# Start addresses of the matrix operands in a two-block transformer kernel: weight tiles at 0 instead of 160, activations of 256 columns at 192 instead of 96 bytes modulo 256

## Chip, cores and metric

The kernel runs on one core of one Trainium2 chip. The metric is the device time of one execution in microseconds (us). Before the change the median of three runs is 2402.97 us (2402.97 to 2404.96).

## What is computed

The reference takes 256 tokens of width 1024 in float32 through two models, one after the other. The first has two layers, each with a feed-forward part, a mixer of three kinds of attention, and a second feed-forward part. The second model has two layers as well, with feed-forward parts, a neighbourhood attention with pooling, and a short convolution; its scale and shift vectors come from a conditioning vector. Cut to what matters here:

```python
D_MODEL, SEQ, D_FF = 1024, 256, 2816

def swiglu(h, w_gu, w_down):
    g, u = jnp.split(h @ w_gu, 2, axis=-1)
    return (jax.nn.silu(g) * u) @ w_down

for l in range(DEPTH):                                  # first model
    x = x + 0.5 * swiglu(rmsnorm(x, g_ffn1[l]), w_ffn1_gu[l], w_ffn1_down[l])
    x = x + hybrid_mixer(rmsnorm(x, g_mix[l]), w_in[l], ...)
    x = x + 0.5 * swiglu(rmsnorm(x, g_ffn2[l]), w_ffn2_gu[l], w_ffn2_down[l])

def ffn_sublayer(h, m, g, w13, w2, base):               # second model
    hn = modulate(rms_norm(h, g), m[:, :, base], m[:, :, base + 1])
    return h + 0.5 * m[:, :, base + 2] * swiglu_2(hn, w13, w2)
```

Eight feed-forward passes make up most of the time: four of the first model, four of the second. One of the second model's handles the 256 tokens and 256 context tokens together.

## The kernel before

**Layout.** Activations stand transposed: the feature lies on the 128 partitions, the 256 tokens (T) in the columns. Each weight block of 128x128 is the stationary operand, and the activations stream past it as the moving operand.

**Three products for one.** Weights and activations are split into a high part of type float32r and the remainder (whi and wlo, h.hi and h.lo). `mm3` (L309 to L313) issues three matmuls per block: high by high (L311), high by low (L312), low by high (L313). With eight blocks of 128 features, one pass over the input takes 24 matmuls. The hidden activations of the feed-forward part are kept in the same way in a tile named A, and those of the mixer in tiles named yy.

**Weights.** They stream from HBM in one order, 1 MB at a time, into three tiles named raw (`load`, L266). ScalarE rounds 1024 columns to whi (L288), VectorE subtracts to give wlo (L291), into four tiles of each. SyncE issues the transfers.

**Stages.** In `ffn`, the gate and up products are written to PSUM tiles named gu, and the down product, with A as the moving operand, to tiles named dn. In the mixers, `tblock` writes tiles named ps. The first model's input has 256 columns. The second model carries the shift vector as two additional columns (TX = 258), so its gu matmuls and part of its ps matmuls stream 258 columns. The joint pass of tokens and context streams 512 columns in dn. VectorE and ScalarE evacuate, and between them VectorE works on a list of dot products for the conditioning (tile mjunk, L553).

**Addresses.** `rows` (L378) makes the tile for an activation: it starts at a multiple of 256 bytes, and its first `at` floats stay unused. With `at` = 24 the data starts at 96 modulo 256. Inside the tile the high and low rows of each block follow each other. A row of 256 columns is 1024 bytes long, so every row starts at 96 modulo 256. A row of 258 columns is 1032 bytes long, so the high row of block k starts at 96 + 16k and the low row at 104 + 16k (k from 0 to 7): the high rows run through 96, 112, 128, 144, 160, 176, 192 and 208. The pool `strm` holds a small tile named one (L1070, L1075, L1076: set to ones and squared once at the start) ahead of raw, whi and wlo. It is 8 floats, 32 bytes, and leaves the tiles behind it at 160 modulo 256. A weight block is 512 bytes, so every block starts at 160 modulo 256 too.

The order of the instructions on each engine is set by a scheduler, from priorities that the code gives; addresses play no part in it.

Of the kernel before, what the change touches and what calls it, by code (L numbers as in the profile page):

```python
# [8 lines left out]
F32 = mybir.dt.float32  # L9
# [7 lines left out]
P = 128  # L17
T = 256
D = 1024
KB = 8  # L20
# [230 lines left out]
class Kern:  # L251
# [123 lines left out]
        nc.vector.tensor_tensor(t, t, v, op=OP.mult)  # L375
        nc.vector.scalar_tensor_tensor(y, t, 1.5, y, op0=OP.add, op1=OP.mult)

    def rows(self, pool, tag, k, n, at=24, **kw):  # L378

        m = 2 * k * n  # L380
        t = pool.tile([P, m + at], F32R, tag=tag, name=tag, align_bytes=256, **kw)
        return t[:, at:].rearrange("p (k s t) -> p k s t", k=k, s=2)

    def newh(self, n=T):
        return self.act(self.rows(self.hpool, "h", KB, n), n)

    def act(self, t, n=T):
        return Act(t[:, :, 0], t[:, :, 1], n, t)
# [662 lines left out]
    def run(self):  # L1051
# [9 lines left out]
        pool = lambda n, b, **k: tc.tile_pool(name=n, bufs=b, **k)  # L1061
        with pool("strm", self.SB) as self.strm, pool("const", 1) as cp, pool("h", 2) as self.hpool, \
# [4 lines left out]
            sc = None  # L1067
            sx.X = cp.tile([P, KB, T], F32, name="X")

            one = self.strm.tile([P, 8], F32, name="one", bufs=1)  # L1070
            self.colt = cp.tile([P, COLSW], F32, name="colt")
            nc.sync.dma_start(self.colt, self.a["cols"])
            self.norm_begin(sx, col("g_ffn1", 0, 8))
# [63 lines left out]
            for l in range(2):  # L1137
                for part in range(2):
# [22 lines left out]
                    n = f"{l}{part}"  # L1161
# [100 lines left out]
```

## Time and profile before

| what | value |
|---|---|
| median of three runs | 2402.97 us |
| the profiled execution's own time | 2412.81 us |
| its span, first to last instruction | 2411.0 us |
| TensorE busy with matmuls | 2375.8 us (99%), 18996 matmuls |
| VectorE busy | 1895.8 us (79%) |
| ScalarE busy | 1183.1 us (49%) |
| GpSimd busy | 185.8 us (8%) |
| weight transfers (queue 1) | 54.6% of 16 engines' span |
| mean granted TensorE clock | 0.996 of full speed |

The profiled execution is 9.8 us (0.4%) above the median of the runs. Matmuls overlap in the profile: one that lasts 282 ns is followed by the next after some 118 ns. So the busy share of TensorE says nothing of its rate. The rate is read from counts: a window of the trace counts every matmul that overlaps it, so the mean interval between two starts is the window plus one duration, divided by the count.

### The profile page before, as it was taken

Reading aid. Unit: us, or ns where it says so; the run is one execution under the profiler, and the core shown is the slowest. Engines: PE = TensorE matmul, PEld = TensorE weight load, DVE = VectorE, ACT = ScalarE, POOL = GpSimd, SP = SyncE. Lnnn points to the kernel's source line nnn. Section 1 sums busy time; section 2 is a strip of 40 time slices with the busy share of each in tenths; the row PEclk is TensorE's granted clock in tenths of the full one; section 3 lists DMA queues with packets and bytes.
Section 4 is the critical chain, followed back from the end, with each engine's and each line's share of the span. In section 5 each row is a group of like instructions: output and inputs, shape, how many; then the busy total and the mean of one; then the engine's idle time right before and its main releaser. Section 6 shows DMA issues by size and latency. Waiting matters only on the chain.

```text
span 2411.0 us, 46263 instructions
## 1 busy us (share of the span) xinstructions
PE 2375.8 (99%) x18996; PEld 2307.1 (96%) x18996; DVE 1895.8 (79%) x3244; ACT 1183.1 (49%) x1803; POOL 185.8 (8%) x283
## 2 busy tenths in 40 slices
PE   8999999999999999999999999999999999999998
PEld 8999899999999989899999899988899999999998
DVE  8876887997897678699787657685799799788773
ACT  5444455544544445465544323435655455545553
POOL 0001103000000110220110000030100000001000
PEclk9999999999999999999999999999999999999999
DMA  7655344675666534466545445353378778655553
GB/s 278 217 200 191 118 158 140 236 234 197 234 227 203 207 119 143 147 237 246 210 171 196 150 156 186 130 173 105 117 280 290 251 259 294 233 187 182 191 178 112
DMA packets 79012, 469.01 MB, mean 195 GB/s; under 512 B 8772, under 2 KB 11120, under 8 KB 33488
## 3 DMA queue, kind: packets, MB, share of 16 engines
q1 hardware_dynamic: 77344, 459.67, 54.6%
q0 software_dynamic: 1168, 5.86, 0.7%
q8 instruction: 149, 2.44, 0.4%
q14 instruction: 63, 0.52, 0.1%
q10 hardware_dynamic: 288, 0.52, 0.1%
HBM read 464.96 MB, written 1.06 MB: 193 GB/s over the span
## 4 chain that ended last, share of the span: by engine, by line
PE 94%; DVE 3%; ACT 2%; issue 1%; POOL 0%; DMA 0%; DVEq 0%; SPq 0%; ACTq 0%; POOLq 0%
PE gu L312 16%; PE gu L313 15%; PE gu L311 15%; PE dn L311 8%; PE dn L312 8%; PE dn L313 8%; PE ps L312 6%; PE ps L311 6%; PE ps L313 6%; PE y L316 2%; PE tok L316 1%; DVE wlo L291 1%; PE sc L316 1%; ACT whi L288 0%; PE zc L316 0%
## 5 line engine op out<-in xcount | busy, mean ns | idle before, releaser
L288 ACT ACTIVATE whi<-raw 128x1024 fp32r<-128x1024 f32 (+2 forms) x717 | 752.4, 1051 | 774.6 <-PE gu L312 271.3
L291 DVE TENSOR_TENSOR wlo<-raw,whi 128x1024 fp32r<-128x1024 f32 (+2 forms) x717 | 873.6, 1220 | 257.2 <-ACT whi L288 254.1
L311 PE MATMUL gu<-h,whi 128*128 128x258 f32 (+1 forms) x3168 | 893.3, 282 | 7.3 <-ACT whi L288 7.3
L312 PE MATMUL gu<-h,whi 128*128 128x258 f32 (+1 forms) x3168 | 896.9, 283 | 0.0
L313 PE MATMUL gu<-h,wlo 128*128 128x258 f32 (+1 forms) x3168 | 893.1, 282 | 0.9 <-DVE wlo L291 0.9
L311 PEld LDWEIGHTS gu<-h,whi 128*128 128x128 f32 x3168 | 598.0, 189 | 7.5 <-ACT whi L288 7.3
L313 PEld LDWEIGHTS gu<-h,wlo 128*128 128x128 f32 x3168 | 602.8, 190 | 1.3 <-DVE wlo L291 1.1
L312 PEld LDWEIGHTS gu<-h,whi 128*128 128x128 f32 x3168 | 600.8, 190 | 0.2
L311 PE MATMUL dn<-A,whi 128*128 128x256 f32 (+1 forms) x1408 | 414.8, 295 | 0.0
L313 PE MATMUL dn<-A,wlo 128*128 128x256 f32 (+1 forms) x1408 | 414.7, 295 | 0.0
L312 PE MATMUL dn<-A,whi 128*128 128x256 f32 (+1 forms) x1408 | 414.3, 294 | 0.0
L311 PE MATMUL ps<-h,whi 128*128 128x256 f32 (+1 forms) x1296 | 371.5, 287 | 9.2 <-DVE ev L917 4.2
L312 PE MATMUL ps<-h,whi 128*128 128x256 f32 (+1 forms) x1296 | 371.8, 287 | 0.1
L313 PE MATMUL ps<-h,wlo 128*128 128x256 f32 (+1 forms) x1296 | 367.7, 284 | 0.0
L312 PEld LDWEIGHTS dn<-A,whi 128*128 128x128 f32 x1408 | 266.1, 189 | 7.8
L313 PEld LDWEIGHTS dn<-A,wlo 128*128 128x128 f32 x1408 | 265.6, 189 | 7.9
L311 PEld LDWEIGHTS dn<-A,whi 128*128 128x128 f32 x1408 | 265.3, 188 | 7.8
L311 PEld LDWEIGHTS ps<-h,whi 128*128 128x128 f32 x1296 | 247.1, 191 | 13.3 <-issue 4.4
L312 PEld LDWEIGHTS ps<-h,whi 128*128 128x128 f32 x1296 | 247.8, 191 | 3.0 <-issue 1.7
L313 PEld LDWEIGHTS ps<-h,wlo 128*128 128x128 f32 x1296 | 248.1, 192 | 0.9 <-issue 0.4
L553 DVE SCALAR_TENSOR_TENSOR mjunk<-mraw,sc 128x1024 bf16<-128x1024 f32 x184 | 225.3, 1224 | 16.6 <-DMA mraw<-modw 16.4
L464 ACT ACTIVATE A<-av 128x256 fp32r<-128x256 f32 x198 | 80.9, 412 | 117.0 <-DVE av L521 58.4
(301 smaller groups left out, 2123.1 us busy)
## 6 DMA issues: line engine op xcount, KB each, us to landing
raw<-wst SPq DMA_DIRECT2D x344, 1024.0 KB, 4.9
mraw<-modw SPq DMA_DIRECT2D x144, 512.0 KB, 4.5
sc<-cc SPq DMA_DIRECT2D x7, 1024.0 KB, 6.8
raw<-wst SPq DMA_DIRECT2D x6, 714.0 KB, 4.1
raw<-wst SPq DMA_DIRECT2D x7, 512.0 KB, 4.4
raw<-wst SPq DMA_DIRECT2D x4, 869.0 KB, 4.5
k<-c POOLq DMA_DIRECT2D x2, 1026.0 KB, 7.5
bt<-rpb SPq DMA_DIRECT2D x8, 256.0 KB, 2.8
```

The lines of the kernel that those rows point to most:

```text
L288: i = nc.scalar.activation(hi[:, :w], raw, AF.Copy)
L291: i = nc.vector.tensor_tensor(lo[:, :w], raw, hi.bitcast(F32)[:, :w], op=OP.subtract)
L311: mm(ps, w[0], x[0], start=start, stop=False)
L312: mm(ps, w[0], x[1], start=False, stop=False)
L313: mm(ps, w[1], x[0], start=False, stop=stop)
L316: self.nc.tensor.matmul(ps, w, x, start=start, stop=stop)
L464: self.nc.scalar.activation(hi, src, AF.Copy)
L553: self.pin(nc.vector.scalar_tensor_tensor(junk, raw, 0.5, self.sc[:, c], op0=OP.mult, op1=OP.mult, accum_out=m[:, idx:idx + 1]))
```

## The change

Three constants change. `rows` leaves 48 floats unused instead of 24, so activations of 256 columns, A and yy start at 192 instead of 96 modulo 256. `newh` leaves 16 for inputs of 258 columns: their high rows start at 64 + 16k instead of 96 + 16k (64 to 176 instead of 96 to 208), their low rows at 72 + 16k instead of 104 + 16k. The tile one grows from 32 to 128 bytes, so all tiles behind it move by 96 bytes, and the weight tiles start at 0 instead of 160 modulo 256. Tiles of other kinds move by 96 bytes as well, except those that are aligned to 256 bytes.

The order of the instructions on every engine stays as it is. Two instructions at the start get larger: the memset and the activation on the tile one work on 32 columns instead of 8.

```diff
-    def rows(self, pool, tag, k, n, at=24, **kw):
+    def rows(self, pool, tag, k, n, at=48, **kw):
 
         m = 2 * k * n
         t = pool.tile([P, m + at], F32R, tag=tag, name=tag, align_bytes=256, **kw)
         return t[:, at:].rearrange("p (k s t) -> p k s t", k=k, s=2)
 
     def newh(self, n=T):
-        return self.act(self.rows(self.hpool, "h", KB, n), n)
+        return self.act(self.rows(self.hpool, "h", KB, n, 48 if n == T else 16), n)
...
-            one = self.strm.tile([P, 8], F32, name="one", bufs=1)
+            one = self.strm.tile([P, 32], F32, name="one", bufs=1)
```

## Rows read from the trace of the kernel before

**Rows 1.** The page: span, TensorE's busy time, and the granted clock by slices
```profile
span 2411.0 us, 46263 instructions
...
PE 2375.8 (99%) x18996; PEld 2307.1 (96%) x18996; DVE 1895.8 (79%) x3244; ACT 1183.1 (49%) x1803; POOL 185.8 (8%) x283
...
PEclk9999999999999999999999999999999999999999
```

**Rows 2.** The page: the chain that ended last, by engine
```profile
PE 94%; DVE 3%; ACT 2%; issue 1%; POOL 0%; DMA 0%; DVEq 0%; SPq 0%; ACTq 0%; POOLq 0%
```

**Rows 3.** Groups by form, TensorE: line, tiles, shape, count | busy, mean | idle before
```profile
L312 PE MATMUL gu<-h,whi 128*128 128x258 f32 x1760 | 499.5, 284 | 0.0
...
L312 PE MATMUL gu<-h,whi 128*128 128x256 f32 x1408 | 397.5, 282 | 0.0
...
L311 PE MATMUL dn<-A,whi 128*128 128x256 f32 x1232 | 345.1, 280 | 0.0
...
L311 PE MATMUL ps<-h,whi 128*128 128x256 f32 x912 | 261.1, 287 | 5.0 <-DVE mt L903 3.8 <-DVE qa L656 1.2
L312 PE MATMUL ps<-h,whi 128*128 128x258 f32 x384 | 111.3, 290 | 0.1
...
L313 PE MATMUL dn<-A,wlo 128*128 128x512 f32 x176 | 69.7, 396 | 0.0
...
L311 PE MATMUL ps<-yy,whi 128*128 128x256 f32 x144 | 40.5, 281 | 1.0 <-DVE mt L903 1.0
```

**Rows 4.** Windows with 256 columns only: stretch, busy and count by engine, clock, DMA
```profile
20.00:120.00 100.00, 100.00 (x851) 100.00 (x851) 90.94 (x141) 52.14 (x75) 0.00 (x0) 1.00 0.71 245
140.00:180.00 40.00, 40.00 (x342) 40.00 (x342) 25.22 (x30) 19.23 (x26) 4.03 (x4) 1.00 0.53 187
...
1080.00:1150.00 70.00, 70.00 (x597) 70.00 (x596) 69.33 (x114) 35.15 (x52) 0.00 (x0) 1.00 0.70 245
1880.00:1920.00 40.00, 40.00 (x356) 40.00 (x355) 30.82 (x44) 19.34 (x27) 4.07 (x5) 1.00 0.75 267
2060.00:2105.00 45.00, 45.00 (x400) 45.00 (x399) 33.81 (x46) 21.16 (x28) 4.03 (x4) 1.00 0.70 251
```

**Rows 5.** Tile dn, 140 to 180 us: count, duration min/median/max, first and last start
```profile
L312 PE MATMUL dn<-A,whi x114: 280/282/282, 139.8 to 179.8; 128*128 128x256 f32 x114
L313 PEld LDWEIGHTS dn<-A,wlo x114: 187/188/188, 139.8 to 179.8; 128*128 128x128 f32 x114
```

**Rows 6.** Tile dn, 1880 to 1920 us
```profile
L312 PE MATMUL dn<-A,whi x119: 275/277/277, 1879.8 to 1919.9; 128*128 128x256 f32 x119
...
L313 PEld LDWEIGHTS dn<-A,wlo x118: 187/188/188, 1880.1 to 1919.9; 128*128 128x128 f32 x118
```

**Rows 7.** Windows: 512 columns (1360 to 1400), 258 columns (1760 to 1860)
```profile
1360.00:1400.00 40.00, 40.00 (x174) 32.27 (x173) 26.86 (x41) 8.22 (x8) 0.00 (x0) 1.00 0.65 229
1760.00:1860.00 100.00, 100.00 (x840) 100.00 (x839) 98.41 (x171) 59.78 (x93) 0.00 (x0) 1.00 0.86 303
```

**Rows 8.** Groups by form, one pass of 258 columns, blocks 0 to 3 (1302.82 to 1304.08)
```profile
L311 PE MATMUL gu<-h,whi 128*128 128x258 f32 x4 | 1.1, 284 | 0.0
L312 PE MATMUL gu<-h,whi 128*128 128x258 f32 x4 | 1.1, 283 | 0.0
L313 PE MATMUL gu<-h,wlo 128*128 128x258 f32 x4 | 1.1, 282 | 0.0
```

**Rows 9.** The same pass, blocks 4 to 7 (1304.255 to 1305.51)
```profile
L312 PE MATMUL gu<-h,whi 128*128 128x258 f32 x4 | 1.1, 284 | 0.0
L313 PE MATMUL gu<-h,wlo 128*128 128x258 f32 x4 | 1.1, 281 | 0.0
L311 PE MATMUL gu<-h,whi 128*128 128x258 f32 x4 | 1.1, 280 | 0.0
```

**Rows 10.** Timeline of the start, ScalarE: start, duration
```profile
2.04 0.21 ACT L1076 ACTIVATE one<-one 128x8 f32<-128x8 f32 x1
...
5.84 0.91 ACT L407 ACTIVATE h<-X,colt 128x256 fp32r<-128x256 f32 x2 [3.59 <-DMA X<-xt]
```

## Prediction

> **What bounds the kernel now.** I read the page first. TensorE is busy for 99% of the span, at a granted clock of nine tenths or more in every slice [rows 1], and 94% of the chain that ended last are its matmuls; DMA has 0% of it [rows 2]. So the time is the number of matmuls times the interval between them, and only what changes this interval counts. Next come the groups by form [rows 3]. Three lines issue one product, so the counts are three times those of a row: 3 x 1408 = 4224 matmuls of 256 columns in gu, 3 x 1232 = 3696 in dn, 3 x (912 + 144) = 3168 in ps, together 11088; 3 x (1760 + 384) = 6432 of 258 columns; 3 x 176 = 528 of 512 columns. They wait for almost nothing: the idle times beside them are a few us.
>
> Then the windows, where the reader is to divide. In the stretch from 20 to 120 us 851 matmuls of 256 columns overlap 100 us, so their interval is 100.28 / 851 = 117.8 ns; 140 to 180 us gives 40.28 / 342 = 117.8. From 1880 to 1920 and 2060 to 2105 us, with the same shape, the same offsets and the same code, it is 40.28 / 356 = 113.1 and 45.28 / 400 = 113.2 [rows 4]. The kernel has **two intervals for the same matmul**, 4.6 ns or 4% apart. The tile dn shows where that sits: a matmul lasts 282 ns in the first kind of stretch and 277 in the second, with hardly any spread, while the weight load lasts 188 in both [rows 5, 6]. The stream of activations is held up for some 5 ns more, the weight load is not. The other engines don't do it: the DMA share is 0.53 from 140 us and 0.75 from 1880 us, VectorE is busy for 63% in the one and 77% in the other [rows 4]. What is left is the place of the operands and the moment at which the stream starts.
>
> **Whether the place matters** is shown by the 258-column passes, the only ones whose rows start at different offsets. Blocks 0 to 3 (high rows at 96 to 144) last 284, 283 and 282 ns on the three lines [rows 8]; blocks 4 to 7 (160 to 208) last 280, 284 and 281 [rows 9]. The two lines that stream the high row (L311, L313) average 283 against 280.5. The weights stand at 160 in all of them. So high rows at 160 to 208 are held up less than at 96 to 144, by about half of the 5 ns that part the two intervals.
>
> **The change, part by part.** No instruction is added, removed or reordered; operands move.
>
> *256 columns, 96 to 192.* The offset leaves the half of the offsets with the long durations for the one with the short ones. No row shows 256 columns at 192, so I bound the gain. One end: every run settles at the short interval. All of gu has the long one today (mean 282), of dn about 60% (its mean of 280 lies 3 of the 5 ns above 277) [rows 3, 5, 6]; of ps, whose means contain waits, I take half. That is 4224 + 2218 + 1584 = 8026 matmuls x 4.6 ns = 36.9 us. The other end: the offset that favours the short interval is left, and the 11088 - 8026 = 3062 matmuls that have it today take the long one, 14.1 us more. I take the first end, since the row nearest to it, the short durations at 160 to 208, lies on its side.
>
> A cover runs out there. From 1080 to 1150 us VectorE is busy for 69.33 of 70 us [rows 4], with the subtractions that make wlo; a faster TensorE waits for it. Of that pass's 1056 gu matmuls x 4.6 = 4.9 us, 1% of 124 us, 1.2, is left: 3.7 us come off. In 20 to 120 us VectorE is at 91%, which leaves room for 4%. The term is **-33 us**.
>
> The Trainium skill, in "TensorE: Matmul & The Clock Gate", section "Back-to-back issue gap", puts the gap of a lone stream at N / 2.4 + 2.5 ns, 109.2 for 256 columns. The trace doesn't reach it in either kind of stretch (113.2 and 117.8); by the rule, if the new offsets freed the stream fully, the term would be an estimated 8026 x 8.6 + 3062 x 4.0 = 81 us before VectorE's limit.
>
> *258 columns, 96 + 16k to 64 + 16k.* Blocks at 192 and 208 disappear, blocks at 64 and 80 come, which no row shows. Three lines of blocks 0 to 3 sum to 849 ns, of 4 to 7 to 845. If the two new offsets behave like the first half, a quarter of 2144 products loses 4 ns: **+2 us**. Bounds: all products like the first half, 2144 x 4 / 2 = +4 us; or the short interval with two columns more (114.0 against 100.28 / 840 = 119.4 [rows 7]), 6432 x 5.4 = -35 us. VectorE, at 98.41 of 100 us from 1760 to 1860 [rows 7], cuts the latter: two of the four passes can gain 1.6%, 4 us instead of 11, so -28 is the end.
>
> *512 columns.* (40 + 0.4) / 174 = 232 ns today [rows 7]. Nothing shows them at 192. Held up 5 ns less, they save 528 x 5 = 2.6 us; I take 0.
>
> *Weights 160 to 0.* Weight loads last 188 ns at either interval [rows 5, 6], and the short interval exists with weights at 160, so I cost it at nothing; if the distance of the two operands matters, it belongs to the rivals. Their transfers now land at 0 modulo 256: DMA is 0% of the chain [rows 2], and there is no cover to lose.
>
> *Tile one and the others.* The activation on one takes 0.21 us at 2.04 us, and ScalarE then waits until 5.84 us for the first input [rows 10]: covered, and without that under 0.2 us. Other tiles move by 96 bytes on engines that hold 5% of the chain [rows 2]: nothing.
>
> Sum: -33 + 2 = -31 us on the profiled execution's 2412.81 us, so 2381.8. That execution stands 9.8 us above the median of the runs, so I forecast 2372 us against 2402.97.
>
> **The rivals.** *Nothing moves.* Where the operands' distance counts rather than each offset, 256 columns stay as they are: weights and activations both move by 96 bytes, and 192 - 0 equals 96 - 160 modulo 256. The 258 columns then change by 32 bytes of offset, worth -2 to +4 us: 2401 to 2407. For it: one distance already shows both intervals, so which one holds could be settled by the moment a run of matmuls starts, and nothing in the change touches that. Against it: the durations of rows 8 and 9 differ by offset, though there the distance varies with it. The Trainium skill's page "SBUF — State Buffer", section "Who interferes with whom", has TensorE wait for no other engine at its own read ports; on that ground an offset would be worth nothing. The trace agrees that the other engines don't set the rate, but it has two intervals all the same.
>
> *Slower: the short interval is lost.* The stretches that have it lie in dn after 258-column passes (1880, 2060 us) [rows 4]. If it hangs on a start that these passes happen to hit, their new offsets shift that start, and the dn passes behind them and half of ps settle at 117.8: +14.1, with +4 of the 258 columns +18, so 2421. It decides once more matmuls go from the short interval to the long one than the other way, and from over 1100 of the 3062 it can be measured (5 us). Against it: nothing says that the long interval is the rule at 192.
>
> *Both shapes gain.* With the 258-column passes near the short interval too, -33 - 28 - 3 = -64: 2339. For it, only that 64 to 176 loses the mixed neighbourhood of 192 and 208 on no evidence; hence a small chance.
>
> *Half of it.* Runs settle differently by their start, as today, but more of them at the short interval: -5 to -24 us.
>
> **How the numbers follow.** What a measurement can tell from no change is 0.2%, 5 us. Forecast (-25 to -45 us) 0.42, both shapes 0.12, half 0.12: faster 0.66. Nothing moves: 0.15. Slower: 0.19. The likeliest is the first, 2372. For 8 in 10 I cut the low end inside the both-shapes case at 2336 and the high end between no change and the full loss at 2411; beyond them I leave some 0.05 and 0.13. The likeliest case alone spans 2358 to 2378.
>
> **What would show it.** Right: windows like 20 to 120 us count about 885 matmuls instead of 851, matmuls of dn last 277 ns in all passes, weight loads still 188, and VectorE has no idle time from 1080 us on while TensorE now waits there for wlo. The 258-column windows stay at 840 per 100 us. Wrong: counts of 851 in gu (nothing moves), or 342 per 40 us in the dn passes near 1880 and 2060 us (short interval lost), or 258-column windows that change by over 2%, which would mean that I had put the effect on the wrong shape.

## The result, and the profile after

The changed kernel takes 2417.78 us (median of four runs, 2414.55 to 2420.98), the kernel before beside it 2403.57 (2402.97 to 2404.96): a ratio of 1.0058 with an interval of 1.0041 to 1.0076. It is **slower** by 14 us, where 2372 us was forecast, and lies above the range. The profiled execution of the change took 2415.88 us. That of before took 2412.81, well above its own median, so the two traces part by 3.07 us alone. The clock, at the end of this section, explains why it is so little; what is left of the 14 us lies in executions without a trace.

TensorE stays the bound (page of the change):

```profile
span 2414.1 us, 46263 instructions
...
PE 2379.9 (99%) x18996; PEld 2310.6 (96%) x18996; DVE 1895.4 (79%) x3244; ACT 1182.9 (49%) x1803; POOL 186.1 (8%) x283
...
PEclk9999999999999999999999999999999999999999
```

So the intervals are the place to look. The windows of the change, with three stretches of [rows 4] and four more (1445 to 1525 and 1760 to 1840 us: 258 columns; 1722 and 2188 us: ps with 256 columns):

```profile
20.00:120.00 100.00, 100.00 (x852) 100.00 (x851) 90.69 (x141) 52.39 (x75) 0.00 (x0) 1.00 0.71 245
140.00:180.00 40.00, 40.00 (x342) 40.00 (x341) 25.39 (x30) 19.18 (x26) 4.03 (x4) 1.00 0.53 185
1445.00:1525.00 80.00, 80.00 (x669) 80.00 (x669) 58.34 (x111) 31.86 (x56) 0.00 (x0) 1.00 0.49 172
1722.00:1734.00 12.00, 12.00 (x100) 11.60 (x99) 9.42 (x16) 7.98 (x15) 1.67 (x2) 1.00 0.32 119
1760.00:1840.00 80.00, 80.00 (x669) 80.00 (x669) 78.59 (x135) 47.01 (x73) 0.00 (x0) 1.00 0.87 309
2060.00:2105.00 45.00, 45.00 (x384) 45.00 (x384) 32.48 (x45) 20.61 (x26) 4.02 (x4) 1.00 0.68 242
2188.00:2203.00 15.00, 15.00 (x129) 15.00 (x128) 11.69 (x20) 7.92 (x14) 1.30 (x2) 1.00 0.50 181
```

The four new stretches in the kernel before:

```profile
1445.00:1525.00 80.00, 80.00 (x672) 80.00 (x671) 58.35 (x111) 32.22 (x56) 0.00 (x0) 1.00 0.49 170
1722.00:1734.00 12.00, 12.00 (x95) 11.43 (x94) 9.39 (x19) 6.94 (x13) 0.10 (x1) 1.00 0.25 89
1760.00:1840.00 80.00, 80.00 (x673) 80.00 (x671) 78.81 (x137) 48.16 (x75) 0.00 (x0) 1.00 0.85 300
2188.00:2203.00 15.00, 15.00 (x134) 15.00 (x134) 12.63 (x20) 8.35 (x15) 2.15 (x3) 1.00 0.48 152
```

Read the counts. The first pass has the long interval as before: 852 and 342 against 851 and 342 [rows 4]. The dn pass near 2060 us counts 384 instead of 400: it went from 113.2 ns to 45.28 / 384 = 117.9. The 258 columns count 669 instead of 672 or 673: from 119.4 to 120.0 ns. The ps run at 2188 us went from the short interval to the long one (134 to 129), that at 1722 us the other way (95 to 100). Tile dn of the change from 1880 to 1920 us (count, duration min/median/max) shows what was 277 ns and x119 in [rows 6]:

```profile
L312 PE MATMUL dn<-A,whi x114: 281/281/281, 1880.0 to 1919.9; 128*128 128x256 f32 x114
```

Adding up the intervals between starts over a trace, gu of 256 columns takes 502.4 us before and 502.5 after; gu of 258 columns 632.0 and 634.8; dn of 256 columns 430.4 and 434.8; 512 columns 123.2 in both. So gu of 256 columns gained nothing, and the losses stand in 258 columns and in dn, 7.2 us together. In ps the traces part the other way, 403.4 and 400.1 us with 256 columns, 149.8 and 149.0 with 258. In the groups by form of the change, beside 499.5, 397.5 and 345.1 us in [rows 3], dn shows it; for 258 columns the overlapping durations hide most of what the counts show:

```profile
L312 PE MATMUL gu<-h,whi 128*128 128x258 f32 x1760 | 499.8, 284 | 0.0
...
L312 PE MATMUL gu<-h,whi 128*128 128x256 f32 x1408 | 397.2, 282 | 0.0
...
L311 PE MATMUL dn<-A,whi 128*128 128x256 f32 x1232 | 346.2, 281 | 0.0
```

Behind this stands the clock. The slices of 60 us on the page hide short falls of the granted clock, which show in narrow windows of the kernel before:

```profile
408.00:418.00 10.00, 8.98 (x64) 8.98 (x65) 6.99 (x13) 5.01 (x9) 3.28 (x3) 0.83 0.29 107
1016.00:1026.00 10.00, 9.36 (x68) 9.36 (x69) 7.19 (x12) 5.00 (x10) 4.02 (x6) 0.83 0.53 205
1618.00:1634.00 16.00, 13.41 (x90) 13.20 (x89) 10.27 (x22) 4.37 (x8) 0.00 (x0) 0.79 0.26 98
```

The change has one of them alone, shorter, and stands at 1.00 near 410 and 1018 us:

```profile
408.00:418.00 10.00, 9.08 (x77) 9.05 (x78) 8.61 (x13) 6.49 (x12) 4.26 (x4) 1.00 0.40 120
1618.00:1634.00 16.00, 13.56 (x100) 13.56 (x101) 10.23 (x20) 5.53 (x10) 0.00 (x0) 0.89 0.19 66
```

All lie in ps stretches, where TensorE also waits. During a fall the granted clock is 0.50, the level of 1.2 GHz instead of 2.4, and the matmuls near 412 us start 213 ns apart instead of 113. The windows give what it cost: (1 - 0.83) x 10 = 1.7 us twice and (1 - 0.79) x 16 = 3.4 us in the trace of before, 6.8 us together, against (1 - 0.89) x 16 = 1.8 us in that of the change. Without this the two traces would part by an estimated 8 us.

### The profile page after: what moved, and what is told of

Read it like the earlier page. It is cut to its first block, busy times and chain, and to the rows that moved or that the text cites. A ratio compares the mean times of both kernels' runs of the same rounds, so it can differ in the third digit from the quotient of the medians.

```text
span 2414.1 us, 46263 instructions
## 1 busy us (share of the span) xinstructions
PE 2379.9 (99%) x18996; PEld 2310.6 (96%) x18996; DVE 1895.4 (79%) x3244; ACT 1182.9 (49%) x1803; POOL 186.1 (8%) x283
## 4 chain that ended last, share of the span: by engine, by line
PE 94%; DVE 3%; ACT 2%; issue 1%; POOL 0%; DMA 0%; DVEq 0%; SPq 0%; ACTq 0%; POOLq 0%
PE gu L312 16%; PE gu L311 16%; PE gu L313 16%; PE dn L311 8%; PE dn L312 8%; PE dn L313 8%; PE ps L312 6%; PE ps L311 6%; PE ps L313 6%; PE y L316 2%; PE tok L316 1%; DVE wlo L291 1%; PE sc L316 1%; ACT whi L288 1%; PE zc L316 0%
## 5 line engine op out<-in xcount | busy, mean ns | idle before, releaser
L312 PE MATMUL gu<-h,whi 128*128 128x258 f32 (+1 forms) x3168 | 897.0, 283 | 0.0
L312 PEld LDWEIGHTS gu<-h,whi 128*128 128x128 f32 x3168 | 598.6, 189 | 0.2
L312 PE MATMUL dn<-A,whi 128*128 128x256 f32 (+1 forms) x1408 | 415.0, 295 | 0.0
L312 PE MATMUL ps<-h,whi 128*128 128x256 f32 (+1 forms) x1296 | 369.8, 285 | 0.1
L312 PEld LDWEIGHTS dn<-A,whi 128*128 128x128 f32 x1408 | 264.2, 188 | 8.0
L312 PEld LDWEIGHTS ps<-h,whi 128*128 128x128 f32 x1296 | 245.8, 190 | 3.0 <-issue 1.7
```

What stands on the lines that cost most here:

```text
L312: mm(ps, w[0], x[1], start=False, stop=False)
```

## Experiments

In all of them the instructions, their data and their order on TensorE are those of before; start addresses differ, and where the tile one grows, the two instructions on it. *Distance* is the start of an activation row minus that of a weight block, modulo 256 bytes. The **short interval** is 113.3 to 113.4 ns, the **long** one 117.8. Intervals are the time between the first and the last start of a stretch, divided by the steps between them.

**Theories.** (A) *The distance counts.* Then the change leaves 256 columns alone (192 before and after) and acts through the 258 columns, whose high rows go from distances 192 + 16k to 64 + 16k. (B) *Each operand's own offset counts*, as the prediction had it. (C) *The weights' offset alone counts.*

### Everything moved by 96 bytes

The change without its special case for 258 columns: weights at 0, all activations 96 bytes further, every distance as before.

```diff
-    def rows(self, pool, tag, k, n, at=24, **kw):
+    def rows(self, pool, tag, k, n, at=48, **kw):
...
-            one = self.strm.tile([P, 8], F32, name="one", bufs=1)
+            one = self.strm.tile([P, 32], F32, name="one", bufs=1)
```

> Weights at 0, all activations at 192 mod 256, the 258-column rows too: both operands of every large matmul stand 96 bytes further on than before, their distance is unchanged. If the distance alone counts: 258 columns at 119.4 ns as before (756 matmuls in 90 us), the dn passes near 1880 and 2060 us at 113.2 ns again (356 in 40 us), time 2403 us, within 5 us. If each operand's own offset counts: 258-column rows at 192 + 16k give another interval than 119.4, and the time lies 5 us or more from 2403.

Measured: 2408.14 us (10 runs) against 2408.02 (16 runs of before), ratio 0.9999 (0.9983 to 1.0014). Windows of this kernel:

```profile
20.00:120.00 100.00, 100.00 (x885) 100.00 (x884) 94.05 (x147) 55.14 (x77) 0.00 (x0) 1.00 0.73 256
1445.00:1525.00 80.00, 80.00 (x672) 80.00 (x671) 56.41 (x107) 32.13 (x56) 0.00 (x0) 1.00 0.49 171
1860.00:1900.00 40.00, 40.00 (x356) 40.00 (x355) 28.83 (x36) 19.15 (x26) 4.03 (x4) 1.00 0.74 264
```

258 columns count 672 and dn behind them has the short interval, as before. A move of both operands by 96 bytes changes nothing that the runs can tell. The first pass, however, has the short interval here (885), with the same distances that gave 851.

### 258 columns alone

Weights and 256 columns as before; only the 258-column rows move, from 96 to 224, which gives them the distances of the change (64 + 16k).

```diff
-        return self.act(self.rows(self.hpool, "h", KB, n), n)
+        return self.act(self.rows(self.hpool, "h", KB, n, 24 if n == T else 56), n)
```

> The kernel before, only the 258-column rows moved to 224 + 16k mod 256, which is the change's distance from the weights (64) with the weights left at 160. If the distance alone counts: 258 columns at 120.0 ns as in the changed kernel, the dn passes behind them at 117.8 (342 in 40 us), time 2412 to 2421 us. If the own offset counts: 258 columns somewhere between 117 and 122 ns but not 120.0, and the dn passes behind them may keep 113.2.

Measured: 2412.85 us (7 runs), ratio 1.0037 (1.0017 to 1.0057). Its windows:

```profile
20.00:120.00 100.00, 100.00 (x885) 100.00 (x884) 93.96 (x148) 55.37 (x77) 0.00 (x0) 1.00 0.73 256
1445.00:1525.00 80.00, 80.00 (x669) 80.00 (x668) 57.52 (x109) 32.48 (x57) 0.00 (x0) 1.00 0.48 169
1860.00:1900.00 40.00, 40.00 (x342) 40.00 (x341) 28.64 (x37) 18.76 (x25) 3.39 (x4) 1.00 0.69 245
2060.00:2105.00 45.00, 45.00 (x384) 45.00 (x384) 32.92 (x44) 21.03 (x28) 4.77 (x5) 1.00 0.67 240
```

This is the main finding. A and the weights stand where they stood in the kernel before, and still dn near 1880 and 2080 us has the long interval (342, 384) instead of the short one (356 and 400 in [rows 4]). What moved is the input of the pass ahead of it. So **the passes of 258 columns settle which of two intervals the 256 columns behind them get**. This edit alone brings the slowdown, as far as the intervals can tell the two apart.

The first pass counts 885 where the kernel before had 851 [rows 4], though nothing up to there differs between the two: there the interval is another one from execution to execution.

### Weights alone

```diff
-            one = self.strm.tile([P, 8], F32, name="one", bufs=1)
+            one = self.strm.tile([P, 32], F32, name="one", bufs=1)
```

Distance 96 for 256 and 512 columns, 96 + 16k for 258.

> The kernel before, only the weights moved to 0 mod 256 (and with them the unaligned tiles by 96 bytes); activations stay at 96. If the activations' own offset counts: as before, 2403 us within 5 us, 258 columns at 119.4 ns. If the distance counts (96 now instead of 192): 258 columns at another interval than 119.4 ns; 256 columns at 113.3 and 117.8 in another mixture, time off 2403 by more than 5 us.

Measured: 2450.5 us (4 runs), ratio 1.0186 (1.0166 to 1.0207). Its windows:

```profile
20.00:120.00 100.00, 100.00 (x836) 100.00 (x835) 89.17 (x139) 51.56 (x74) 0.00 (x0) 1.00 0.70 245
1445.00:1525.00 80.00, 80.00 (x665) 80.00 (x664) 56.61 (x106) 32.12 (x56) 0.00 (x0) 1.00 0.42 147
2060.00:2105.00 45.00, 45.00 (x376) 45.00 (x375) 35.48 (x56) 23.65 (x35) 0.26 (x1) 1.00 0.64 232
```

256 columns take 100.28 / 836 = 120.0 ns in all gu and dn passes, not the mixture of two intervals that was expected, and 258 columns take 120.8. The weights' move alone, which the prediction cost at nothing, is worth 42 us. Weights at 0 were no loss in the first experiment, so theory C falls as well: the distance counts.

### Three scans of the distance

One kernel holds several distances, one for each pass; the rows of `h` and A get lists of offsets. The edit of the first scan (weights at 0), cut to its core; the second has weights at 160, the third at 32, with other lists:

```diff
+        self.HT, self.HX, self.AO, self.np = [0, 48, 48, 8, 16, 48, 48, 24, 48, 48], [0, 0, 16, 16, 8, 24, 16, 32], [32, 40, 56, 0, 0, 8, 16, 24], -1
...
+        return self.act(self.rows(self.hpool, "h", KB, n, (self.HT if n == T else self.HX).pop(0)), n)
...
+                    t = self.rows(fp, "A", 11, len(S) * T, self.AO[self.np], bufs=2 // len(S)).rearrange(
```

> Weights at 0; each feed-forward pass has its own offset: gu of 256 columns at 0, 32, 64, 96 mod 256, dn at 128, 160, 224, 0, 32, 64, 96 in the order of the passes (512 columns at 0), gu of 258 columns at 0, 32, 96 and 128 (+ 16k). If the offset or distance sets the interval of 256 columns, the passes differ from 117.8 and 113.3 ns. If it is only the moment at which a run starts, every 256-column pass has one of these two. For 258 columns each pass shows one point of the curve, between 114 and 122 ns.

> Weights at 160 as before; distances (activation minus weight, mod 256) that the first scan left out. gu of 256 columns at distances 176, 208, 184 and 200, dn at 16, 48, 240, 176, 208, 184 and 200 in the order of the passes, 512 columns at 32, gu of 258 columns at 160, 224, 176 and 208 (+ 16k). If the distance alone counts, the curve of the first scan continues: 256 columns between 113.3 and 120.0 ns everywhere, near 192 a neighbour that has the short interval of 113.3 alone is possible; 512 columns at 32 below 233.3 as at 0 (226.8). If the own offset counted after all, the weights' return to 160 would break the continuation.

> Weights at 32 mod 256; more distances: gu of 256 columns at 24, 8, 112 and 16, dn at 80, 144, 188, 196, 8, 24 and 40 in the order of the passes, 512 columns at 240, gu of 258 columns at 240, 224, 16 and 8 (+ 16k). If the distance alone counts, 16 gives 116.7 ns again though the weights stand elsewhere, and every stretch lies between 113.3 and 120.0. If 192 is a single narrow place with the short interval, 188 and 196 lie near 120.0 as 184 and 200 do.

Measured: 2420.2, 2424.45 and 2422.85 us, one run each. Windows of gu at distance 0 (first scan, 20 us), of gu at 112 and dn at 196 (third scan, 640 and 1160 us):

```profile
20.00:120.00 100.00, 100.00 (x835) 100.00 (x835) 89.21 (x139) 51.51 (x74) 0.00 (x0) 1.00 0.69 245
```

```profile
640.00:720.00 80.00, 80.00 (x708) 80.00 (x708) 75.35 (x117) 43.40 (x61) 0.00 (x0) 1.00 0.71 242
...
1160.00:1220.00 60.00, 60.00 (x496) 60.00 (x495) 42.77 (x57) 29.57 (x44) 10.83 (x11) 1.00 0.53 190
```

That is 120.1, 80.28 / 708 = 113.4 and 60.28 / 496 = 121.5 ns. All intervals, with 96 and 192 from the runs above:

| distance, 256 columns | interval, ns |
|---|---|
| **112** | **113.4** |
| 192 | 113.3 or 117.8 |
| 32, 144 | 116.7 |
| 16 | 116.7 (dn), 118.7 (gu) |
| 160, 240 | 117.3, 117.2 |
| 64 | 117.8 |
| 8 | 117.8 (dn), 120.0 (gu) |
| 48, 80, 224 | 118.3 |
| 128, 188 | 118.7, 118.5 |
| 40, 176, 208 | 119.3, 119.3, 119.2 |
| 0, 24, 96, 184, 200 | 120.0 |
| 196 | 121.7 |

258 columns, by the distance of block 0: 119.2 at 0, 16, 208 and 240, 119.5 at 192 (before), 119.7 at 8, 32, 160 and 224, 120.0 at 64 (the change) and 176, 120.5 at 128, 120.8 at 96. 512 columns: 226.8 at 0, 233.3 at 32, 96 and 192, 236.5 at 240. One distance gives one interval in passes far apart (gu and dn at 0 both 120.0), with 8, 16 and 192 as exceptions. At 8 and 16 the gu passes of the third scan begin with some 35 matmuls at 117.8 and 116.8 ns, the intervals of dn there, and go over to 120.0 and 118.7 behind a break in the stream of matmuls; so these two look like 192, distances with two intervals. No simple rule shows in the table. Steps of 4 or 8 bytes beside 192 cost up to 8 ns. Three things came out otherwise than expected: 512 columns at 32 stayed at 233.3 ns, 16 gave 118.7 in gu instead of 116.7 again, and 188 and 196 gave 118.5 and 121.7 instead of 120.0.

### The change once more, and distance 112 everywhere

The change is run once more, unaltered, together with a kernel built from the table: weights at 128, 256 columns at distance 112, 512 columns at 0, 258 columns at 208 + 16k.

```diff
-    def rows(self, pool, tag, k, n, at=24, **kw):
+    def rows(self, pool, tag, k, n, at=60, **kw):
...
+        self.HT, self.HX, self.AO, self.np = [60, 60, 60, 60, 60, 60, 60, 60, 60, 60], [20, 20, 20, 20, 20, 20, 20, 20], [60, 60, 60, 60, 32, 60, 60, 60], -1
...
-            one = self.strm.tile([P, 8], F32, name="one", bufs=1)
+            one = self.strm.tile([P, 64], F32, name="one", bufs=1)
```

> The changed kernel once more, beside the kernel before on the same chip, because the kernel before ran from 2401 to 2411 us in the comparison of the first experiments. If the loss comes from the 258-column passes (0.57 ns x 6432 = 3.6 us) and the two dn passes behind them (1056 x 4.4 ns = 4.7 us), the ratio lies near 1.0035 (8 us), with 258 columns at 120.0 ns and the dn passes near 1880 and 2060 us at 117.8 ns again. If the rest of the first 14 us is part of the change, the ratio stays near 1.006.

> Weights at 128; all activations of 256 columns at distance 112, 512 columns at distance 0, 258-column rows at distance 208 + 16k: the best stretches of the three scans put together. If the distance sets the interval and 112 has the short one alone: 113.4 ns in all 256-column passes (851 becomes 884 matmuls in 100 us), 226.8 for 512 columns and 119.2 for 258; against the kernel before some 8000 x 4.4 ns = 35 us, less what VectorE holds back, plus 3 and 2 us: 2365 to 2380 us. If 112 has two intervals like 192 and the one scan happened to show the short one: 2390 to 2410 us, with passes at 113.4 and others at a longer interval.

Measured: the change 2414.36 us (8 runs) against 2405.22 (13 runs), ratio 1.0040 (1.0025 to 1.0055). Distance 112: **2373.72 us** (4 runs), ratio 0.9865 (0.9845 to 0.9886), faster than both kernels. Windows of the repeated change, then of distance 112 (1040: gu of 256 columns, 1720: 258 columns, 1840: dn of 256):

```profile
20.00:120.00 100.00, 100.00 (x885) 100.00 (x884) 93.61 (x148) 55.16 (x77) 0.00 (x0) 1.00 0.73 256
1870.00:1910.00 40.00, 40.00 (x342) 40.00 (x341) 27.56 (x35) 18.59 (x25) 4.04 (x4) 1.00 0.70 253
```

```profile
20.00:120.00 100.00, 100.00 (x885) 100.00 (x884) 93.84 (x148) 55.26 (x77) 0.00 (x0) 1.00 0.73 255
1040.00:1120.00 80.00, 80.00 (x706) 79.94 (x705) 79.33 (x130) 39.03 (x58) 0.00 (x0) 1.00 0.70 246
1720.00:1800.00 80.00, 80.00 (x674) 80.00 (x673) 78.81 (x136) 47.98 (x75) 0.00 (x0) 1.00 0.78 288
1840.00:1880.00 40.00, 40.00 (x355) 40.00 (x354) 29.41 (x37) 19.12 (x25) 4.05 (x4) 1.00 0.71 254
```

The change has the short interval in its first pass this time (885, against 852 in its first trace), and the long one behind the 258 columns again (342). At distance 112 some 10000 of the 11088 matmuls of 256 columns have the short interval, against some 2700 before. Their intervals add up to 32.4 us less (gu 502.4 to 484.3, dn 430.4 to 420.3, ps 403.4 to 399.2); 512 columns go from 233.3 to 226.7 ns (3.5 us) and gu of 258 columns from 632.0 to 630.5 (1.5 us). Sum 37 us; the two profiled executions part by 2412.81 - 2375.56 = 37.3, the medians by 31.5. The medians part by less, since the traced execution of before lies above its median.

TensorE's only wait for wlo from VectorE, first in the kernel before, then at distance 112 (us in total, times, longest), lies in both within the first 20 us:

```profile
PE gu L313 <- DVE wlo L291: 0.9, 1, 0.9
```

```profile
PE gu L314 <- DVE wlo L292: 1.0, 1, 1.0
```

## Why the prediction was wrong

**What bounds the kernel: right.** Matmuls times their interval, 113.2 and 117.8 ns for one and the same matmul (4.4 ns apart by starts, where the counts gave 4.6). The kernel with distance 112 gained what its intervals say. One reading on the way was not whole: the weight load that lasts 188 ns in both kinds of stretch [rows 5, 6] is that of one line of three. That of L312 lasts 192 ns from 140 to 180 us and 188 from 1880 to 1920:

```profile
L312 PEld LDWEIGHTS dn<-A,whi x114: 191/192/193, 140.1 to 180.0; 128*128 128x128 f32 x114
```

```profile
L312 PEld LDWEIGHTS dn<-A,whi x118: 187/188/188, 1880.0 to 1919.8; 128*128 128x128 f32 x118
```

So in the long interval one load in three is held up too. Which of the two holds up the other is not shown.

***"Whether the place matters"* is the step that failed.** It read the shorter durations of blocks 4 to 7 [rows 9] as those of high rows at 160 to 208, and said that the weights stand at 160 in all of them. With fixed weights, offset and distance vary together, so rows 8 and 9 could not tell them apart; the rival *nothing moves* said so, and the forecast went by the offset anyway. The first experiment settles it: offsets moved together, nothing measured (ratio 0.9999). The distance does matter (113.4 to 121.7 ns), so that a place matters at all was right. The change keeps it at 192 for 256 columns.

***256 columns, 96 to 192*, -33 us: measured 0 in gu** (502.4 and 502.5 us) **and a loss of 4.4 us in dn.** The 852 of the first pass and the 342 of dn near 1880 us are counts that the prediction named as signs of being wrong. The 852 proves little, though: that pass counts 885 in the repeated change, and in the second experiment, where nothing up to there differs from before.

***Weights at nothing*: wrong as an edit of its own** (+42 us). Together with the activations' move of the same 96 bytes it leaves the distance of 256 columns where it was.

***258 columns*, +2 us: right in sign and near in size, by luck.** 2.8 us in gu by the two traces, 0.53 ns for each of 5280 matmuls; with those of ps, 6432 x 0.53 = 3.4 us, inside the bounds of -28 to +4. But the sum was made of offsets, and what changed is the distance.

***512 columns*, 0: right** (233.3 ns in both), though taken without a reason; their distance stayed at 192.

**The slower rival was the right mechanism, and its price too large.** It said that the dn passes behind the 258 columns have the short interval by a start which those passes hit. The second experiment shows the dependence: those passes' rows moved, and dn with unmoved operands followed. The two traces with 258 columns at distance 192 + 16k (the kernel before, and all moved) agree in the 256-column stretches behind them, and so do the three at 64 + 16k (the change twice, 258 alone) but for two at the end. The table has the stretches of 40 matmuls and more; one of 65 in the last dn, short in all five, is left out:

| stretch, start in before | matmuls | at 192 + 16k | at 64 + 16k |
|---|---|---|---|
| ps, 1730 us | 135 | long | short |
| dn, 1872 us | 528 | short | long |
| dn, 2059 us | 528 | short | long |
| ps, 2190 us | 192 | short | long |
| last dn, 2338 us | 132 | short | long |
| last dn, 2353 us | 86 | long | short |
| last dn, 2371 us | 45 | short | long |
| last dn, 2378 us | 140 | long | short in the change, long with 258 alone |
| last dn, 2395 us | 45 | short | short in the change, long with 258 alone |

The scans bear it out where their 256 columns stand at 192: behind 64 + 16k (first scan) the two ps stretches are short and long, behind 192 + 16k (second scan) long and short.

In the change 1425 matmuls lose the short interval there and 361 win it: 1064 x 4.4 = 4.7 us. With 3.4 us of the 258 columns the loss is 8.1 us, a ratio of 1.0034. The spans say the same. From the first matmul of 258 columns to the end the kernel before takes 1184.2 us and all moved 1181.7, the change 1190.8 and 1191.0, 258 alone 1191.4. Less what the low clock cost there (3.4 and 0 us, and 1.8 in each of the last three) the two groups lie at 1180.8 and 1181.7 against 1189.0 to 1189.6, 8.0 us apart on average. The ratio lies inside the intervals of the repeat (1.0025 to 1.0055) and of 258 columns alone (1.0017 to 1.0057), below that of the first comparison (1.0041 to 1.0076). The rival's +18 put all of the 3062 short matmuls at the long interval; those ahead of the first 258 columns don't follow it. That a start settles the interval fits too: in the five traces that have 256 columns at 192 throughout, runs of one interval go over to the other some 150 times, and each time a step of 170 ns or more, a break in the stream or a stretch at the low clock, lies between.

**The rival that nothing moves** had the distance right, and 256 columns ahead of the first 258 did as it said. It gave 2401 to 2407 us because it took the passes for independent of each other.

**What stays open.** Ahead of 1030 us several stretches take either interval from execution to execution at the same addresses. The first pass, with the dn behind it, was long in the traces of before and of the change, and short in the other three with distance 192; it is worth (1015 + 528) x 4.4 = 6.8 us. The 16 times of before beside the first three experiments lie half at 2402 to 2407 and half at 2409 to 2411 us, which this would fit, and the clock does not tell the halves apart (mean granted clock 0.9978 and 0.9974, worth 1 us). But timed runs leave no trace, so that the rest of the 14 us is of this kind is argued, not shown. The clock is a rival for a part of it: in the repeat it was 0.9969 for the change and 0.9979 for before, on average, which would be worth some 2 us. Whether the change has a hand in that is open. Nor do the runs show how a pass settles the next one, or why the distance counts.

**VectorE's cover: priced too high.** In the gu pass from 1040 us TensorE was to wait 3.7 of the 4.9 us for wlo. The change did not put this to the test, but distance 112 did: the pass, from the first start of gu to the first of dn, went from 125.1 to 120.6 us, and TensorE waits for no wlo in it. VectorE is busy for 79.33 of 80 us there all the same, but 22 us of the pass are dot products (tile mjunk), for which no matmul of it waits. A busy share near 100% was not a limit here.

**The gap of a lone matmul.** The Trainium skill, in "TensorE: Matmul & The Clock Gate", section "Back-to-back issue gap", puts that of 256 columns at 109.2 ns. No stretch of any run reaches it: the shortest interval is 113.3 ns. The -81 us that the rule would give were not there at any distance tried.

## What to carry to other kernels

Where matmuls follow each other without waits, read the interval by stretch from counts, and try the start of the moving operand against that of the stationary one modulo 256 bytes: it was worth from -1.3% to +1.9% here, with no other edit. Moving both operands by 96 bytes did nothing, so work an address change out in distances before making anything of offsets. One trace at an address with two intervals proves little about that address; take one whose stretches agree in every pass. Before two traces are compared by their times, look for stretches at a lower clock.

## What the runs showed of the hardware

- The interval of a 128x128 by 256 matmul (float32r) ran from 113.3 to 121.7 ns with the distance of its operands, at a granted clock of 1.00, which is the level of 2.4 GHz. 512 columns ran from 226.7 to 236.5.
- At distance 192 the same addresses gave 113.3 or 117.8 ns, held for whole passes of up to a thousand matmuls and more; in five traces it never changed without a step of 170 ns or more between. At 112 every pass of the faster kernel settled at the short one; behind a break some ten matmuls ran at about 118 ns first.
- A pass's interval can depend on the addresses of the pass ahead of it (second experiment: dn at 117.8 ns instead of 113.4, its own operands unmoved).
- The granted clock fell to 0.50, the level of 1.2 GHz, in ps stretches of some executions, at a cost of 1.7 to 3.4 us each, and stood at 1.00 in the same stretches of others.
